# A bias table read back in four parts through GpSimd's queue, and key norm roots formed earlier

## The chip, the cores and the metric

The kernel runs on one core of one Trainium2 chip. The core has five engines that run side by side, each through its own list of instructions in a fixed order: TensorE (PE, matmuls; its weight loads are shown as PEld), VectorE (DVE), ScalarE (ACT), GpSimd (POOL) and SyncE (SP, which in this kernel only issues DMA transfers). They wait for one another by semaphores. The metric is device time in microseconds (us) of one launch, the median of three runs.

## The reference, cut to what matters

The program is a decoder trunk of two layers over 256 tokens of 1024 channels, all in float32. Layer 0 mixes tokens by a state-space scan (S5); then one set of keys and values is made; layer 1 mixes by attention that reads them. Around each mixer stand two feed-forward blocks (SwiGLU), four in all:

```python
for layer in range(DEPTH):                       # DEPTH = 2
    h = h + 0.5 * swiglu(rmsnorm(h, ffn1_norm), w_in, w_out)
    h = h + mixer(rmsnorm(h, mix_norm))          # S5 in layer 0, attention in layer 1
    h = h + 0.5 * swiglu(rmsnorm(h, ffn2_norm), w_in, w_out)
    if layer == 0:
        kv = rmsnorm(h, kv_norm) @ w_kv          # (256, 6, 4, 64)
        k_cmp = rmsnorm(compress(kv[:, 0])); v_cmp = compress(kv[:, 1])
        k_slc = rmsnorm(kv[:, 2]); k_win = rmsnorm(kv[:, 4])   # v: kv[:, 3], kv[:, 5]
```

Attention adds to its logits a bias that depends only on the head (16) and on the distance of two tokens, `rel_bias[bucket(distance), head]`, and masks negative distances.

## The kernel before, in words

**Weights.** Every product is a float32 product done in three passes (lines 126 to 128): weights are loaded as 1 MB granules `raw` (line 76, always on SP, two buffers), ScalarE writes the rounded part `whi` (line 92 without, line 105 with a gain) and VectorE the rest `wlo` (lines 96 and 108). Each granule is two halves; five halves of `whi` and five of `wlo` have room. A `raw` buffer is free for the next load when VectorE has read it for the last time, and a half is free when TensorE has done with it.

**A feed-forward block** (`ffn`) goes through 11 chunks of 256 hidden columns. In each TensorE does 48 passes of 512 columns into `mm` (two granules of `w_in`), four transposes of the previous chunk's `g` (line 265, into a bank `tr` that ScalarE and VectorE empty into `turned`, lines 151 and 152), then ScalarE and VectorE form `g` (lines 306 and 307) and TensorE does 24 passes into `o` with one granule of `w_out`. From the second such chunk on this is a period of 72 passes.

**Background work.** Four times in a chunk and once after it, `background` lets a generator go on by one step; a step may say with `yield 4` that it counts for four. In the second feed-forward block of layer 0 the generators are `kv_consts` and `bias_tables`; in the first of layer 1 it is `post`, which makes the transposed keys. The order in which the instructions of such a block stand on each engine is set when the kernel is built, by a scheduler with its own estimate of every instruction and transfer; it is fixed at run time. Only the S5 part and the attention have an order written out by hand.

**The bias table.** `bias_tables` makes `rev`, for 128 rows a reversed table of 384 distances (line 833, a matmul with one-hot rows; lines 835 and 836). It writes `rev` twice to a scratch `revd` in DRAM (line 840), and reads it back eight times with a step that shifts each row by one (line 846), into `B` (128 x 16 heads x 256). Both are issued by SP, between the loads of `raw`. `B` is first read in the attention (line 1153).

**The keys.** `post` first transposes the compressed branch's inputs `kd` in four steps (line 917: four transposes each, emptied by VectorE at line 919 and by ScalarE at line 921 or 923). Then, for the two other branches (`n` = 1, 2) and two halves of the tokens (`t`), it squares `kt` on GpSimd (`sq`, line 853), sums on VectorE (`hss`, 855), scales (`hms`, 861), takes the root on GpSimd (`hrr`, 863), multiplies on VectorE (`kn`, 929), applies the gain on GpSimd (`kd2`, shown as `kd`, 932) and transposes (936). `sq`, `kn` and `kd2` have one buffer each; `hss`, `hms` and `hrr` have one too.

Of the kernel before, what the change touches and what calls it, by code (L numbers as in the profile page):

```python
# [9 lines left out]
F32 = mybir.dt.float32  # L10
# [6 lines left out]
P = 128  # L17
# [6 lines left out]
EPS = 1e-6  # L24
# [8 lines left out]
def kernel(ctx: ExitStack, tc: tile.TileContext, A, out):  # L33
# [791 lines left out]
    def bias_tables(kp, tp):  # L825

        rb = tp.tile([32, P], F32, name="rb")
        nc.sync.dma_start(out=rb, in_=A["rel_bias"])
        oh = tp.tile([32, 256], F32, name="oh")
        nc.sync.dma_start(out=oh, in_=A["bucket"])  # L830
        yield
        ps = tr_bank()
        T.matmul(ps[:, 0:256], lhsT=rb, rhs=oh, start=True, stop=True)
        rev = tp.tile([P, 384], F32, name="rev")
        G.memset(rev[:, 256:384], -1e30)
        V.tensor_copy(rev[:, 0:256], ps[:, 0:256])
        yield
        dr = dscr.tile([16, 16, 384], F32, name="revd")
        for r in range(2):
            nc.sync.dma_start(out=dr[8 * r:8 * r + 8].rearrange("q h k -> (q h) k"), in_=rev)  # L840
            yield
        yield
        KV.B = kp.tile([P, 16, 256], F32, name="B")
        for r in range(8):
            src = bass.AP(tensor=dr.tensor, offset=dr.offset + 127 - 16 * r, ap=[[16 * 384 - 1, 16], [384, 16], [1, 256]])
            nc.sync.dma_start(out=KV.B[16 * r:16 * r + 16], in_=src)
            yield 4

    def head_ss(tp, x, nh):

        rows = x.shape[0]
        sq = tp.tile([P, 384], F32, name="sq")[:rows, :nh * 64]
        G.tensor_tensor(out=sq, in0=x, in1=x, op=ALU.mult)
        ss = tp.tile([P, 8], F32, name="hss")[:rows, :nh]
        V.tensor_reduce(out=ss, in_=sq.rearrange("p (h d) -> p h d", d=64), axis=mybir.AxisListType.X, op=ALU.add)
        return ss

    def inv_sqrt(tp, ss, scale, eps):
        rows, n = ss.shape
        ms = tp.tile([P, 8], F32, name="hms")[:rows, :n]  # L860
        V.tensor_scalar(out=ms, in0=ss, scalar1=scale, scalar2=eps, op0=ALU.mult, op1=ALU.add)
        rr = tp.tile([P, 8], F32, name="hrr")[:rows, :n]
        G.tensor_tensor(out=rr, in0=ms, in1=nhalf[:rows, :n], op=ALU.pow)
# [18 lines left out]
    def shared_kv(x, kp, tp):  # L882
# [26 lines left out]
        def post():  # L909
            w1 = tp.tile([P, 16, P], F32, name="cw1")  # L910
            nc.sync.dma_start(out=w1, in_=A["cmp_k_w1"])
            kvT = KV.kvT
            for t in range(2):
                for i in range(2):
                    ps = tr_bank()
                    for g in range(4):
                        T.transpose(ps[:, g * P:(g + 1) * P], kd[t][:, i * 4 + g].rearrange("p a d -> p (a d)"), ident)
                    pv = ps.rearrange("p (g c) -> p g c", g=4)
                    V.tensor_copy(kvT[i][0:64, 0:4, t * P:(t + 1) * P], pv[0:64])
                    if t == 0:  # L920
# [4 lines left out]
            for n in (1, 2):  # L925
                for t in range(2):
                    rr = inv_sqrt(tp, head_ss(tp, kt[n, t], 4), 1.0 / 64, EPS)
                    kn = tp.tile([P, 4, 64], F32, name="kn")
                    V.tensor_tensor(out=kn, in0=kt[n, t].rearrange("p (g d) -> p g d", g=4), in1=rr.unsqueeze(2).to_broadcast([P, 4, 64]), op=ALU.mult)
                    kd2 = tp.tile([P, 4, 2, 64], F32, name="kd2")  # L930
# [43 lines left out]
            yield  # L974
            rr = inv_sqrt(tp, head_ss(tp, kc, 1), 1.0 / 64, EPS)
            kcd = tp.tile([60, 2, 64], F32, name="kcd")
            for u in range(2):
# [421 lines left out]
def _arrays(np, I):  # L1399
# [20 lines left out]
    A["w_glu"] = _w_out(I["s5_w_glu"][0])  # L1420
    A["rel_bias"] = np.tile(I["rel_bias"], (1, 8))
    n = np.arange(255, -1, -1)
# [47 lines left out]
```

## Time and profile before

| what | value |
|---|---|
| median of three runs | 998.76 us (998.57 to 1000.18) |
| the profiled execution's own time | 1000.22 us |
| its span in the trace | 998.5 us |
| TensorE busy, of the span | 969.4 us (97%) |
| VectorE, ScalarE, GpSimd busy | 659.0, 577.1, 80.6 us |
| granted TensorE clock | full (2.4 GHz) over the whole span |
| DMA moved | 168.96 MB, mean 169 GB/s |

The profile shows one execution; its own time stands 1.46 us over the median, and its span 1.72 us under its own time. Matmuls overlap in the records (each is shown with 0.39 us, and the next starts 0.23 us after it), so a busy TensorE is not one at its peak: what tells a slow stretch is the length of a chunk, and the idle time ahead of single weight loads. Stretches are given in us from the span's start: the second feed-forward block of layer 0 lies at some 270 to 460, the keys' product and the first block of layer 1 at 460 to 700, the attention at 700 to 820.

### The profile page before, as it was taken

To read this page: it belongs to the slowest core of one execution; us is meant where nothing else is said; L and a number is where in the kernel's file an instruction comes from. 1 tells how busy PE (TensorE), PEld (TensorE's weight loads), DVE (VectorE), ACT (ScalarE), POOL (GpSimd) and SP (SyncE) were. 2 spreads that over 40 slices of the span, in tenths; PEclk is the share of its full clock that TensorE was granted. 3 is DMA by queue.
4 is the path that set the end of the run, shared out by engine and by line. 5 is a ranking of instruction groups with operands and counts; after the bars stand their busy time and mean duration, and the time that the engine had idled before them with its cause. 6 is when DMAs were issued, how large, how long until landed. Compare 5 with 4: busy or idle time off the path is not lost.

```text
span 998.5 us, 14337 instructions
## 1 busy us (share of the span) xinstructions
PE 969.4 (97%) x5523; PEld 794.1 (80%) x5523; DVE 659.0 (66%) x1210; ACT 577.1 (58%) x1023; POOL 80.6 (8%) x91
## 2 busy tenths in 40 slices
PE   6999999999999989999999999999988999999998
PEld 5788788788878867788878888888876778888886
DVE  4998875579964544657566556565899676555553
ACT  5677666463663543656656545454888565555552
POOL 3001012312200000000032000000200000000000
PEclk9999999999999999999999999999999999999999
DMA  7555565433357556564644445554431235555551
GB/s 270 192 192 202 174 208 177 164 94 146 97 190 212 158 174 216 185 228 151 248 169 166 170 171 197 182 189 135 127 107 43 85 127 211 193 186 185 195 179 74
DMA packets 28948, 168.96 MB, mean 169 GB/s; under 512 B 4560, under 2 KB 7184, under 8 KB 10064
## 3 DMA queue, kind: packets, MB, share of 16 engines
q1 hardware_dynamic: 28656, 167.26, 49.7%
q8 instruction: 43, 0.70, 0.3%
q0 software_dynamic: 224, 0.79, 0.2%
q14 instruction: 25, 0.20, 0.1%
HBM read 165.54 MB, written 2.49 MB: 168 GB/s over the span
## 4 chain that ended last, share of the span: by engine, by line
PE 78%; DVE 11%; ACT 5%; DMA 4%; issue 1%; POOL 1%; SPq 0%; ACTq 0%
PE mm L126 15%; PE mm L127 15%; PE mm L128 14%; PE o L128 7%; PE o L127 7%; PE o L126 7%; DMA raw<-in_w_in_dram 3%; DVE wlo L96 3%; PE tr L265 2%; ACT whi L92 1%; DVE Pt L1153 1%; PE dr L596 1%; PE tr L945 1%; PE ga L126 1%; PE ga L128 1%
## 5 line engine op out<-in xcount | busy, mean ns | idle before, releaser
L126 PE MATMUL mm<-whi,xT 128*128 128x512 f32 (+2 forms) x800 | 312.4, 392 | 6.1 <-ACT whi L92 2.6
L127 PE MATMUL mm<-wlo,xT 128*128 128x512 f32 (+2 forms) x800 | 306.3, 383 | 0.7 <-DVE wlo L96 0.5
L128 PE MATMUL mm<-whi,xT 128*128 128x512 f32 (+2 forms) x800 | 305.9, 383 | 0.0
L108 DVE SCALAR_TENSOR_TENSOR wlo<-raw,gains,whi 128x512 fp32r<-128x512 f32 x274 | 192.7, 748 | 86.7 <-ACT whi L105 84.1
L105 ACT ACTIVATE whi<-raw,gains 128x512 fp32r<-128x512 f32 x274 | 182.6, 718 | 98.8 <-PE mm L128 50.1
L96 DVE TENSOR_TENSOR wlo<-raw,whi 128x1024 fp32r<-128x1024 f32 x132 | 160.5, 1224 | 104.4 <-ACT whi L92 103.8
L92 ACT ACTIVATE whi<-raw 128x1024 fp32r<-128x1024 f32 x132 | 138.4, 1059 | 121.5 <-PE mm L128 51.5
L126 PEld LDWEIGHTS mm<-whi,xT 128*128 128x128 f32 x800 | 150.7, 189 | 37.1 <-ACT whi L105 3.1
L127 PEld LDWEIGHTS mm<-wlo,xT 128*128 128x128 f32 x800 | 151.1, 189 | 29.4 <-DVE wlo L96 1.5
L128 PEld LDWEIGHTS mm<-whi,xT 128*128 128x128 f32 x800 | 150.7, 188 | 29.3
L128 PE MATMUL o<-whi,turned 128*128 128x512 f32 x352 | 137.5, 391 | 0.8 <-DVE turned L152 0.8
L127 PE MATMUL o<-wlo,turned 128*128 128x512 f32 x352 | 137.6, 391 | 0.1
L126 PE MATMUL o<-whi,turned 128*128 128x512 f32 x352 | 136.8, 391 | 0.0
L128 PEld LDWEIGHTS o<-whi,turned 128*128 128x128 f32 x352 | 66.1, 188 | 15.0 <-DVE turned L152 1.5
L127 PEld LDWEIGHTS o<-wlo,turned 128*128 128x128 f32 x352 | 66.1, 188 | 14.4 <-DVE wlo L96 1.0
L126 PEld LDWEIGHTS o<-whi,turned 128*128 128x128 f32 x352 | 66.0, 188 | 13.7
L306 ACT ACTIVATE g<-mm,rs 128x256 f32<-128x256 f32 x88 | 41.0, 472 | 45.2 <-PE mm L128 44.9
L307 DVE SCALAR_TENSOR_TENSOR g<-mm,rs,g 128x256 f32<-128x256 f32 x88 | 41.7, 482 | 36.2 <-ACT g L306 36.1
L152 DVE TENSOR_TENSOR turned<-tr,turned 128x512 fp32r<-128x512 f32 x44 | 30.3, 688 | 36.1 <-ACT turned L151 35.7
L151 ACT ACTIVATE turned<-tr 128x512 fp32r<-128x512 f32 x44 | 26.1, 593 | 45.9 <-PE tr L265 45.9
L148 POOL TENSOR_TENSOR rs<-ms,nhalf 128x1 f32<-128x1 f32 x12 | 7.6, 633 | 284.4 <-DVE ms L147 284.4
L1160 ACT ACTIVATE Pt<-Pt,mx 128x128 f32<-128x128 f32 (+1 forms) x64 | 28.3, 446 | 3.7 <-DVE mx L1153 3.7
(321 smaller groups left out, 982.0 us busy)
## 6 DMA issues: line engine op xcount, KB each, us to landing
raw<-in_w_in_dram SPq DMA_DIRECT2D x87, 1024.0 KB, 4.9
raw<-in_w_out_dram SPq DMA_DIRECT2D x44, 1024.0 KB, 4.9
raw<-in_w_kv_dram SPq DMA_DIRECT2D x6, 1024.0 KB, 4.8
raw<-in_w_glu_dram SPq DMA_DIRECT2D x4, 1024.0 KB, 4.9
raw<-in_w_o_dram SPq DMA_DIRECT2D x4, 1024.0 KB, 5.0
raw<-in_w_qg_dram SPq DMA_DIRECT2D x6, 512.0 KB, 3.6
B<-revd SPq DMA_DIRECT2D x8, 256.0 KB, 7.5
raw<-in_w_qg_dram SPq DMA_DIRECT2D x2, 608.0 KB, 3.8
```

What stands on the lines that cost most here:

```text
L92: Last.act = S.activation(hi, r, AF.Copy)
L96: Last.dve = V.tensor_tensor(out=lo, in0=r, in1=hi.bitcast(F32), op=ALU.subtract)
L105: Last.act = S.activation(hi[:, c], r[:, c], AF.Identity, scale=g_)
L108: i = V.scalar_tensor_tensor(out=lo[:, c], in0=r[:, c], scalar=g_, in1=hi[:, c].bitcast(F32), op0=ALU.mult, op1=ALU.subtract)
L126: T.matmul(ps, lhsT=xh, rhs=wh, start=start, stop=False)
L127: T.matmul(ps, lhsT=xh, rhs=wl, start=False, stop=False)
L128: Last.pe = T.matmul(ps, lhsT=xl, rhs=wh, start=False, stop=stop_)
L151: i = S.activation(dst_hi, src, AF.Copy)
L152: V.tensor_tensor(out=dst_lo, in0=src, in1=dst_hi.bitcast(F32), op=ALU.subtract)
L306: Last.act = S.activation(sl, acc[t][:, 0:256], AF.Silu, scale=rs[:, t:t + 1])
L307: Last.dve = V.scalar_tensor_tensor(out=g[:, t, :], in0=acc[t][:, 256:512], scalar=rs[:, t:t + 1], in1=sl, op0=ALU.mult, op1=ALU.mult)
L1160: S.activation(p_, p_, AF.Exp, scale=-1.0, bias=mx[g, t][:, c:c + 1], accum_out=sm[g, t][:, c:c + 1])
```

## The change

Three edits, the first in `bias_tables`:

```diff
-        dr = dscr.tile([16, 16, 384], F32, name="revd")
-        for r in range(2):
-            nc.sync.dma_start(out=dr[8 * r:8 * r + 8].rearrange("q h k -> (q h) k"), in_=rev)
-            yield
-        yield
         KV.B = kp.tile([P, 16, 256], F32, name="B")
-        for r in range(8):
-            src = bass.AP(tensor=dr.tensor, offset=dr.offset + 127 - 16 * r, ap=[[16 * 384 - 1, 16], [384, 16], [1, 256]])
-            nc.sync.dma_start(out=KV.B[16 * r:16 * r + 16], in_=src)
-            yield 4
+        for n in range(4):
+            dr = dscr.tile([16, 4, 384], F32, name=f"revd{n}")
+            for q in range(2):
+                nc.sync.dma_start(out=dr[8 * q:8 * q + 8].rearrange("q h k -> (q h) k"), in_=rev[32 * n:32 * n + 32])
+            for r in range(8):
+                src = bass.AP(tensor=dr.tensor, offset=dr.offset + 127 - 16 * r, ap=[[4 * 384 - 1, 16], [384, 4], [1, 256]])
+                nc.gpsimd.dma_start(out=KV.B[16 * r:16 * r + 16, 4 * n:4 * n + 4], in_=src)
+                yield
```

The scratch becomes four scratches of four heads each. Each is written by two transfers of 48 KB on SP and read back by eight transfers of 64 KB on GpSimd's queue: 8 writes and 32 reads in place of 2 writes and 8 reads, with the same bytes. The rows of `rel_bias` are put in the order that this needs when the inputs are prepared. The second edit is in `post`, and gives `hss`, `hms` and `hrr` four buffers (`bufs=4`):

```diff
-            kvT = KV.kvT
+            kvT, root = KV.kvT, {}
             for t in range(2):
                 for i in range(2):
+                    root[i + 1, t] = inv_sqrt(tp, head_ss(tp, kt[i + 1, t], 4), 1.0 / 64, EPS)
                     ps = tr_bank()
...
-                    V.tensor_copy(kvT[i][0:64, 0:4, t * P:(t + 1) * P], pv[0:64])
+                    placed = V.tensor_copy(kvT[i][0:64, 0:4, t * P:(t + 1) * P], pv[0:64])
...
-                    rr = inv_sqrt(tp, head_ss(tp, kt[n, t], 4), 1.0 / 64, EPS)
                     kn = tp.tile([P, 4, 64], F32, name="kn")
-                    V.tensor_tensor(out=kn, in0=kt[n, t].rearrange("p (g d) -> p g d", g=4), in1=rr.unsqueeze(2).to_broadcast([P, 4, 64]), op=ALU.mult)
+                    with tc.issue_after(placed.ins):
+                        V.tensor_tensor(out=kn, in0=kt[n, t].rearrange("p (g d) -> p g d", g=4), in1=root[n, t].unsqueeze(2).to_broadcast([P, 4, 64]),
+                                        op=ALU.mult)
```

The four roots are formed in the four steps of the first transposes, and every `kn` stands behind the last `kvT` copy. The third edit adds one `yield` between the root of the compressed key and the products that use it, so that its transpose comes a step later.

As the scheduler sets the order, the change moves other instructions too. The first place is ScalarE's list in the second feed-forward block of layer 0, three chunks from the third row of `g` (L306) on. Before:

```order
L306 ACTIVATE g<-mm,rs 128x256 x2
L105 ACTIVATE whi<-raw,gains 128x512 x4
L151 ACTIVATE turned<-tr 128x512
L105 ACTIVATE whi<-raw,gains 128x512 x4
L92 ACTIVATE whi<-raw 128x1024 x2
L306 ACTIVATE g<-mm,rs 128x256 x2
L151 ACTIVATE turned<-tr 128x512
L105 ACTIVATE whi<-raw,gains 128x512 x8
L306 ACTIVATE g<-mm,rs 128x256 x2
L92 ACTIVATE whi<-raw 128x1024 x2
L151 ACTIVATE turned<-tr 128x512
L105 ACTIVATE whi<-raw,gains 128x512 x8
```

The same place now:

```order
L306 ACTIVATE g<-mm,rs 128x256 x2
L105 ACTIVATE whi<-raw,gains 128x512 x4
L92 ACTIVATE whi<-raw 128x1024 x2
L105 ACTIVATE whi<-raw,gains 128x512 x2
L151 ACTIVATE turned<-tr 128x512
L105 ACTIVATE whi<-raw,gains 128x512 x2
L306 ACTIVATE g<-mm,rs 128x256 x2
L105 ACTIVATE whi<-raw,gains 128x512 x4
L92 ACTIVATE whi<-raw 128x1024 x2
L105 ACTIVATE whi<-raw,gains 128x512 x2
```

The order now has one pattern for every chunk, the same as in the other feed-forward blocks; before, `turned` (L151) stood at another place in almost every chunk, ahead of up to eight `whi`. VectorE's list follows ScalarE's line by line.

The second place is SP's list in the same block, from the first write of the scratch on (`raw` are the weight granules):

```order
-L840 DMA revd<-rev 128x384 x2
+L842 DMA revd_3058<-rev 32x384 x2
 L76 DMA raw<-in_w_in_0_dram 128x2048
-L846 DMA B<-revd 16x16x256 x2
+L842 DMA revd_3256<-rev 32x384 x2
+L76 DMA raw<-in_w_out_0_dram 128x2048
+L76 DMA raw<-in_w_in_0_dram 128x2048 x2
 L76 DMA raw<-in_w_out_0_dram 128x2048
 L76 DMA raw<-in_w_in_0_dram 128x2048
-L846 DMA B<-revd 16x16x256
+L842 DMA revd_3470<-rev 32x384 x2
 L76 DMA raw<-in_w_in_0_dram 128x2048
```

The reads of `B` have left this list; the four writes of the scratch stand apart from each other.

The third place is VectorE's list in the first block of layer 1, from the second `g` of its first chunk on (here with the buffers' numbers, since rows read alike without them). Before:

```order
L307 SCALAR_TENSOR_TENSOR g_4603<-mm_4526,rs_4188,g_4603 128x256
L919 COPY kvT0_2925<-tr_4610 64x4x128
L855 TENSOR_REDUCE hss_4725<-sq_4723 128x4
L96 TENSOR_TENSOR wlo_4744<-raw_4741,whi_4743 128x1024
L861 TENSOR_SCALAR hms_4727<-hss_4725 128x4
L919 COPY kvT1_2926<-tr_4639 64x4x128
L929 TENSOR_TENSOR kn_4731<-kt__4423,hrr_4729 128x256
L96 TENSOR_TENSOR wlo_4760<-raw_4741,whi_4759 128x1024
L855 TENSOR_REDUCE hss_4784<-sq_4782 128x4
L861 TENSOR_SCALAR hms_4786<-hss_4784 128x4
L929 TENSOR_TENSOR kn_4790<-kt__4426,hrr_4788 128x256
L919 COPY kvT0_2925<-tr_4664 64x4x128
```

The same place now, from the row behind that `g` on:

```order
L854 TENSOR_REDUCE hss_4645<-sq_4643 128x4
L919 COPY kvT0_2925<-tr_4651 64x4x128
L860 TENSOR_SCALAR hms_4647<-hss_4645 128x4
L854 TENSOR_REDUCE hss_4682<-sq_4680 128x4
L96 TENSOR_TENSOR wlo_4801<-raw_4798,whi_4800 128x1024
L860 TENSOR_SCALAR hms_4684<-hss_4682 128x4
L919 COPY kvT1_2926<-tr_4688 64x4x128
L854 TENSOR_REDUCE hss_4715<-sq_4713 128x4
L96 TENSOR_TENSOR wlo_4817<-raw_4798,whi_4816 128x1024
L860 TENSOR_SCALAR hms_4717<-hss_4715 128x4
L854 TENSOR_REDUCE hss_4757<-sq_4755 128x4
L860 TENSOR_SCALAR hms_4759<-hss_4757 128x4
```

The next row now is the third `kvT` copy. Two `kn` have gone from ahead of it to behind the fourth one, and two more pairs of `hss` and `hms` stand ahead of it.

## Rows read from the trace of the kernel before

**Rows 1.** The page: busy time of each engine over the span, and the share of each engine in the chain of work that ended last.

```profile
PE 969.4 (97%) x5523; PEld 794.1 (80%) x5523; DVE 659.0 (66%) x1210; ACT 577.1 (58%) x1023; POOL 80.6 (8%) x91
PE 78%; DVE 11%; ACT 5%; DMA 4%; issue 1%; POOL 1%; SPq 0%; ACTq 0%
```

**Rows 2.** Busy time by stretch, each stretch one chunk from the second `g` on ScalarE to the next chunk's: the stretch and its length, busy us (and instructions) of each engine, granted clock, mean DMA share, GB/s. Six chunks of the second block of layer 0, and one of the first block of layer 1.

```profile
327.82:344.63 16.81, 16.81 (x77) 13.86 (x76) 9.53 (x14) 8.48 (x14) 0.00 (x0) 1.00 0.47 160
344.63:363.36 18.73, 17.38 (x77) 13.86 (x76) 9.43 (x14) 8.47 (x14) 0.00 (x0) 1.00 0.73 203
363.36:382.08 18.72, 17.33 (x76) 13.48 (x74) 6.96 (x12) 6.45 (x11) 0.00 (x0) 1.00 0.58 201
382.08:400.56 18.48, 17.66 (x76) 13.82 (x76) 9.32 (x14) 8.36 (x13) 0.00 (x0) 1.00 0.71 195
400.56:419.06 18.50, 17.72 (x77) 14.19 (x78) 11.69 (x16) 10.37 (x16) 0.00 (x0) 1.00 0.63 205
419.06:435.87 16.81, 16.81 (x77) 13.91 (x76) 12.04 (x18) 10.93 (x18) 0.00 (x0) 1.00 0.61 217
603.76:620.55 16.79, 16.79 (x77) 13.91 (x76) 9.78 (x14) 8.94 (x14) 0.00 (x0) 1.00 0.54 188
```

**Rows 3.** Timeline of the weight loads in the long chunks, those with idle time ahead of them: start, us, engine, line, operation, output and input, count, and in brackets the idle time and what ended it.

```profile
357.21 0.30 PEld L126 LDWEIGHTS mm<-whi,xT 128*128 128x128 f32 x2 [1.53 <-ACT whi L105]
357.99 0.19 PEld L127 LDWEIGHTS mm<-wlo,xT 128*128 128x128 f32 x1 [0.49 <-DVE wlo L108]
...
382.45 0.14 PEld L265 LDWEIGHTS tr<-ident,g 128*128 128x128 f32 x1 [0.83 <-DVE g L307]
```

**Rows 4.** Timeline of ScalarE in the first two of the long chunks, columns as in rows 3.

```profile
347.19 2.57 ACT L105 ACTIVATE whi<-raw,gains 128x512 fp32r<-128x512 f32 x4 [2.09 <-DMA raw<-in_w_in_dram]
355.95 0.60 ACT L151 ACTIVATE turned<-tr 128x512 fp32r<-128x512 f32 x1 [6.19 <-PE tr L265]
356.44 2.56 ACT L105 ACTIVATE whi<-raw,gains 128x512 fp32r<-128x512 f32 x4
```

**Rows 5.** The reads of `B` and the transfers: the instructions of line 846 from 299 to 400 us (duration min/median/max in ns, first and last start), and from the page the issues by tile (count, KB each, median us from issue to landing).

```profile
L846 SPq DMA_DIRECT2D B<-revd x8: 383/425/441, 305.2 to 395.7; - x8
...
raw<-in_w_in_dram SPq DMA_DIRECT2D x87, 1024.0 KB, 4.9
...
B<-revd SPq DMA_DIRECT2D x8, 256.0 KB, 7.5
...
WBT<-in_s_b_dram POOLq DMA_DIRECT2D x1, 512.0 KB, 7.4
...
revd<-rev SPq DMA_DIRECT2D x2, 192.0 KB, 4.4
```

**Rows 6.** Timeline of GpSimd: the only two transfers that it issues, and its first instruction behind the second block of layer 0.

```profile
7.60 0.74 POOL L435 DMA_DIRECT2D WBT<-in_s_b_dram  x1
8.35 0.55 POOL L436 DMA_DIRECT2D WBT<-in_s_gain_dram  x1
...
469.94 0.55 POOL L148 TENSOR_TENSOR rs<-ms,nhalf 128x1 f32<-128x1 f32 x1 [191.94 <-DVE ms L147]
```

**Rows 7.** A chunk of the first block of layer 1: SP's loads in the timeline, the use of a `w_out` granule by ScalarE, and the time from issue to landing (min/median/max) of the loads of line 76 from 586 to 690 us, then of those from 299 to 320 us.

```profile
587.13 0.33 SPq L76 DMA_DIRECT2D raw<-in_w_out_dram  x1
...
593.09 1.06 ACT L92 ACTIVATE whi<-raw 128x1024 fp32r<-128x1024 f32 x1 [1.38 <-PE o L128]
...
DMA to landing us min/median/max: 3.6/4.8/5.1
...
DMA to landing us min/median/max: 5.7/5.9/7.5
```

**Rows 8.** Timeline of VectorE in the first block of layer 1, from the second `g` of its first chunk on.

```profile
511.48 0.68 DVE L919 COPY kvT<-tr 64x512 f32<-64x512 f32 x1
512.08 0.40 DVE L855 TENSOR_REDUCE hss<-sq 128x4 f32<-128x256 f32 x1
512.41 1.21 DVE L96 TENSOR_TENSOR wlo<-raw,whi 128x1024 fp32r<-128x1024 f32 x1
...
515.27 0.42 DVE L929 TENSOR_TENSOR kn<-kt__4423,hrr 128x256 f32<-128x256 f32 x1 [0.54 <-POOL hrr L863]
...
517.20 0.27 DVE L861 TENSOR_SCALAR hms<-hss 128x4 f32<-128x4 f32 x1
519.71 0.43 DVE L929 TENSOR_TENSOR kn<-kt__4426,hrr 128x256 f32<-128x256 f32 x1 [2.25 <-POOL hrr L863]
520.05 0.68 DVE L919 COPY kvT<-tr 64x512 f32<-64x512 f32 x1
```

**Rows 9.** Timeline of GpSimd in the same stretch.

```profile
512.63 1.49 POOL L853 TENSOR_TENSOR sq<-kt__4426 128x256 f32<-128x256 f32 x1 [24.12 <-DVE hss L855]
514.22 1.02 POOL L863 TENSOR_TENSOR hrr<-hms,nhalf 128x4 f32<-128x4 f32 x1
515.78 2.36 POOL L932 TENSOR_TENSOR kd<-kn,kg 128x256 f32<-128x256 f32 x2 [0.54 <-DVE kn L929]
518.09 0.61 POOL L853 TENSOR_TENSOR sq<-kt__4507 128x256 f32<-128x256 f32 x1
```

**Rows 10.** The weight load of the fourth set of transposes, and ScalarE's part of the third copy, in the timelines of these two.

```profile
521.41 0.42 PEld L917 LDWEIGHTS tr<-ident,kd 128*128 128x128 f32 x4 [1.73 <-ACT kvT L923]
...
520.76 0.60 ACT L923 ACTIVATE kvT<-tr 64x512 f32<-64x512 f32 x1 [2.86 <-DVE kvT L919]
```

More of the change, by code (lines that the diff above doesn't have):

```diff
@@ L853, in head_ss @@
         G.tensor_tensor(out=sq, in0=x, in1=x, op=ALU.mult)
-        ss = tp.tile([P, 8], F32, name="hss")[:rows, :nh]
+        ss = tp.tile([P, 8], F32, name="hss", bufs=4)[:rows, :nh]
         V.tensor_reduce(out=ss, in_=sq.rearrange("p (h d) -> p h d", d=64), axis=mybir.AxisListType.X, op=ALU.add)
@@ L859, in inv_sqrt @@
         rows, n = ss.shape
-        ms = tp.tile([P, 8], F32, name="hms")[:rows, :n]
+        ms = tp.tile([P, 8], F32, name="hms", bufs=4)[:rows, :n]
         V.tensor_scalar(out=ms, in0=ss, scalar1=scale, scalar2=eps, op0=ALU.mult, op1=ALU.add)
-        rr = tp.tile([P, 8], F32, name="hrr")[:rows, :n]
+        rr = tp.tile([P, 8], F32, name="hrr", bufs=4)[:rows, :n]
         G.tensor_tensor(out=rr, in0=ms, in1=nhalf[:rows, :n], op=ALU.pow)
@@ L975, in post @@
             rr = inv_sqrt(tp, head_ss(tp, kc, 1), 1.0 / 64, EPS)
+            yield
             kcd = tp.tile([60, 2, 64], F32, name="kcd")
@@ L1420, in _arrays @@
     A["w_glu"] = _w_out(I["s5_w_glu"][0])
-    A["rel_bias"] = np.tile(I["rel_bias"], (1, 8))
+    A["rel_bias"] = np.tile(I["rel_bias"].reshape(32, 4, 1, 4), (1, 1, 8, 1)).reshape(32, 128)
     n = np.arange(255, -1, -1)
```

## The prediction, made before the result was known

> **What bounds the kernel now.** The page comes first: TensorE is busy for 97% of the span and carries 78% of the chain that ended last [rows 1]. A change can gain only where TensorE waits or starts late; the other engines' time is free unless TensorE comes to wait for it. As a busy TensorE is no proof of its pace, I next cut the feed-forward blocks into chunks and compared lengths [rows 2]. An undisturbed chunk takes 16.79 us. In the block that reads the bias table back, the chunks at 327.82 and 419.06 take 16.81, but the four between them take 18.73, 18.72, 18.48 and 18.50, together 74.43. Four undisturbed ones are 4 x 16.79 = 67.16, so 7.27 us are lost there, with the granted clock at full speed in all of them.
>
> Then the timeline of the weight loads, to see what TensorE waited for. In the first long chunk it is whi for 1.53 us and wlo for 0.49; in the third it begins with 0.83 on g [rows 3]. ScalarE's timeline tells why: it ended four whi at 349.76, then stood 6.19 us in front of turned, waiting for TensorE's transposes of g, with four more whi behind that instruction [rows 4]. These began at 356.44, which is where TensorE ran dry. So it is the fixed order, not the transfers, that makes these waits. The order listing agrees: before, turned stands ahead of up to eight whi, and at another place in almost every chunk.
>
> The second loss lies in the first block of layer 1. TensorE's fourth set of transposes waited 1.73 us for ScalarE's part of the third kvT copy, which had waited for VectorE's part [rows 10]; VectorE had stood 2.25 us before the second kn, for a root on GpSimd [rows 8].
>
> **The change part by part.** *The order of the second block of layer 0.* With the reads of B off SP's list, every chunk has the order of the chunk of 16.79 us. Term: -7.27 us. From both sides: at best each long chunk falls to 16.79, which is that figure; at worst the new order stalls as the old one did and the term is 0. I take 7.27, because the pattern is the one whose length a row shows.
>
> *SP's list.* The eight reads leave it: 8 x 0.425 = 3.4 us of SP's time [rows 5], and none of TensorE's waits [rows 3] is for a transfer. Six more writes come: at that price 2.6 us. The first write waits for rev as before; the loads of raw behind it are the same. I take 0.
>
> *GpSimd's list.* 32 transfers are issued there. The two that the trace shows took 0.74 and 0.55 us to issue [rows 6], so 17.6 to 23.7 us in all. Nothing else stands on GpSimd until the norm of the next block at 469.94, after 191.94 us of idling [rows 6], so there is room. The first write of the scratch goes out at about 300 us, a little ahead of the first read of B at 305.2 [rows 5]; the last one stands eleven loads later in SP's list, which at three loads per chunk of 16.79 is 62 us, at 362. Each part waits for its write, 4.4 us as before [rows 5], and then come eight issues of at most 0.74 us and a landing of 7.4 us [rows 5]: 18 us for a part. So the last part is done at 380, 90 us early. B is first used in the attention. Cost 0 on the path; without that cover the norm would come late by what is missing.
>
> *The loads of raw beside the parts.* The bytes are the same, but a part now comes beside the loads on a queue of its own. Undisturbed, a load lands in 4.8 us; beside the reads of B, from 299 to 320 us, in 5.7 to 7.5 [rows 7]. The margin: a granule issued at 587.13 lands some 4.8 later, at 591.9, and is first read at 593.09, 1.2 us later [rows 7]. Behind that stand the halves of whi and wlo already made. The nearest row is the chunk at 327.82, which follows those slow loads and still took 16.81 [rows 2]. So 0 here; the other bound is in the rivals. Below nothing it cannot go, since the chunk at 16.79 has no wait left to lose.
>
> The Trainium skill ("DMA: Bandwidth & Descriptors", section "Issuing engines are not separate DMA queues") speaks against the change: transfers from any engine run on the same 16 DMA engines, and a second issuing engine saves only the time of issuing. By that rule alone the first edit would be worth nothing, since SP's issue time bounds no chunk here; what the rule would do with the whole sum stands with the third rival.
>
> *The roots.* Time from the second g to the third kvT copy on VectorE. Before: the first kvT began at 511.48 and the third at 520.05 [rows 8]. Now there stand ahead of the third: two kvT of 0.68, four hss of 0.40, two wlo of 1.21 and four hms of 0.27, in all 6.46; from 511.48 that gives 517.9 if nothing waits. Two kn (0.42 and 0.43) and the waits 0.54 and 2.25 go. New waits: each hss wants a sq, and there is one buffer for it. Between the second hss and the third, GpSimd takes a root (1.02) and a sq (0.61, or 1.49 beside a wlo [rows 9]): 1.6 to 2.5 us; VectorE has 1.21 + 0.27 + 0.68 = 2.2 us of work meanwhile. Between the third and the fourth, again a root and a sq, part of them already done, against 1.5 us of work. So VectorE waits 0 to 0.3, then 0 to 1.0 us, and the third copy begins at 517.9 to 519.2, 0.8 to 2.1 us earlier. TensorE's wait of 1.73 falls by as much, at most to nothing. I take 1.5, nearer the full wait, as only the sq beside a wlo is the slow one. Behind it the second kn waits for GpSimd's products of the first (2.36 us for two [rows 9]) against 0.7 of wlo, so g comes late by at most 1.7 us. TensorE has 24 passes into o to do in between, some 5.6 us at the pace of a chunk (72 passes in 16.79, transposes included). That covers it. The bounds of this term: a gain of 1.73, and a loss of the same size if VectorE's new waits outgrow the old ones.
>
> The Trainium skill ("SBUF — State Buffer", section "Who interferes with whom") says that a VectorE instruction with two SBUF inputs, as wlo is, and a GpSimd one that reads SBUF shut each other out. The trace agrees where sq took 1.49 us beside a wlo and 0.61 alone [rows 9]; with every sq so slowed this term would be 0.8 and the time 0.7 us longer.
>
> *The yield* moves one small transpose by a step: 0.
>
> Sum: 7.27 + 1.5 = 8.8 us. The profiled execution took 1000.22 us (span 998.5), so one like it would take 991.4. It stands 1.46 above the median of the runs; taken from that median, 998.76 - 8.8 = 990.0 us.
>
> **The rivals.** *The roots gain nothing.* VectorE's waits for sq and roots are as long as the one removed: 998.76 - 7.3 = 991.5; at the bound of a loss of 1.7 it is 993.2. For it: four sq through one buffer, on an engine that shared badly with wlo. Against: what VectorE does between them is about as long.
>
> *The bursts cost part of it.* The first two writes stand one load apart in SP's list, so 16 issues fall into one chunk or two. If VectorE stood still while GpSimd issues, 16 x 0.74 = 11.8 us would come on top of its 9.78 us of work in a chunk of 16.79 [rows 2]: 4.8 us too many, once. The other parts add 5.9 to 9.78, which fits. That gives 992.3 to 994.8, say 993.5. For it: no row shows a GpSimd transfer beside wlo. Against: VectorE is idle for 7 us of a chunk.
>
> *The change doesn't do what it says.* The long chunks come from B's bytes, which stay, and not from the order: a load did make ScalarE wait 2.09 us in the first of them [rows 4]. Then only the roots gain: 998.76 - 1.5 = 997.3. This is where the skill's rule on issuing engines leads if the order is no cause. Against: the chunk at 327.82 ran beside or right behind slow loads without loss, and the wait at 355.95 was for transposes with no load in sight.
>
> *Slower: the reads starve the loads.* A part is in flight for some 5.9 + 7.4 = 13 us, in which up to three loads are issued (three in 16.79). If each lands in 7.5 instead of 4.8 and nothing is caught up, each is 2.7 - 1.2 = 1.5 late: 4.5 per part, 18 for four, and the time is 990.0 + 18 = 1008. It decides from 8.8 / 4 = 2.2 us per part on. For it: the new queue is not behind the loads but beside them. Against: ScalarE and VectorE idle for 7 us or more in each chunk, in which they catch up.
>
> **How the numbers follow.** Chances: the forecast 0.56, the roots gain nothing 0.17, the bursts 0.15, no effect of the order 0.07, slower 0.05. The forecast's own range is 989.0 to 991.5: with 0.8 to 1.73 for the roots the sum gives 990.7 to 989.8, and the runs of before spread by 1.6, half of it to each side. The range for 8 in 10 takes in the first two rivals above, and half a microsecond below, for waits elsewhere that an earlier arrival may shorten: 988.5 to 995.5. A measurement here can tell some 0.2%, 2 us. The forecast and the first two rivals are faster by more than that, 0.88; no effect of the order is within it, 0.07; the starved loads are slower, 0.05.
>
> **What would show it.** Right: every chunk from 311 to 453 us at 16.8, no idle time of ScalarE ahead of turned above 1 us, GpSimd's issues at under 0.8 us and done before 385, and the fourth set of transposes with under 0.4 us of wait. Wrong: chunks of over 17 us where a part is in flight, with a wait for raw or wlo (bursts or starved loads); long chunks at the same places (bytes, not order); or a VectorE that waits for sq ahead of the third kvT copy.

## The result, and the profile after

The changed kernel takes 989.69 us (median of 4 runs, 988.65 to 991.26) against 998.66 for the kernel before in the same comparison (4 runs, 998.27 to 1000.18): a ratio of 0.9909, with a 95% interval of 0.9897 to 0.9921. It is 9.0 us faster; 8.8 had been forecast. The profiled execution of after took 989.46 us; its span is 987.7, 10.8 us shorter than that of before. Of this 1.0 us lies ahead of the second block of layer 0, where the change edits nothing (the first g of its second chunk stands at 310.36 us before and at 309.37 after); the four executions of before alone spread by 1.9.

The page of after, the two lines that answer to [rows 1]:

```profile
PE 964.6 (98%) x5523; PEld 793.6 (80%) x5523; DVE 662.1 (67%) x1210; ACT 580.6 (59%) x1023; POOL 95.9 (10%) x123
PE 82%; DVE 9%; ACT 5%; DMA 2%; issue 1%; POOL 0%; SPq 0%; DVEq 0%; ACTq 0%
```

Busy time by stretch in after, the chunks of the second block of layer 0 that answer to [rows 2] (stretch and length, busy us and instructions of PE, PEld, DVE, ACT, POOL, granted clock, DMA share, GB/s):

```profile
326.84:343.62 16.78, 16.78 (x77) 13.90 (x76) 9.76 (x14) 8.93 (x13) 4.05 (x8) 1.00 0.72 220
343.62:360.41 16.79, 16.79 (x77) 13.90 (x76) 9.77 (x14) 8.94 (x14) 0.00 (x0) 1.00 0.56 193
360.41:377.20 16.79, 16.79 (x77) 13.90 (x76) 9.77 (x14) 8.94 (x14) 4.05 (x8) 1.00 0.75 225
377.20:393.98 16.78, 16.78 (x77) 13.91 (x76) 9.76 (x14) 8.93 (x13) 0.00 (x0) 1.00 0.55 188
393.98:410.77 16.79, 16.79 (x77) 13.90 (x76) 9.77 (x14) 8.94 (x14) 0.00 (x0) 1.00 0.54 187
```

Every chunk is now the undisturbed one, the two with eight GpSimd issues in them too (POOL 4.05 us): TensorE's busy time is the whole length of each. The four long chunks of [rows 2] held 7.27 us more than that. ScalarE's timeline, against the 6.19 us of [rows 4]:

```profile
339.51 0.60 ACT L151 ACTIVATE turned<-tr 128x512 fp32r<-128x512 f32 x1 [0.46 <-PE tr L265]
356.30 0.60 ACT L151 ACTIVATE turned<-tr 128x512 fp32r<-128x512 f32 x1 [0.46 <-PE tr L265]
```

It reaches turned 0.46 us before the transposes are through. GpSimd's timeline shows the four parts and the first instruction behind them, where [rows 6] has 191.94 us of idling:

```profile
303.33 4.14 POOL L845 DMA_DIRECT2D B<-revd  x8 [26.32 <-DMA revd<-rev]
311.47 4.05 POOL L845 DMA_DIRECT2D B<-revd  x8 [4.01 <-DMA revd<-rev]
337.87 4.05 POOL L845 DMA_DIRECT2D B<-revd  x8 [22.34 <-DMA revd<-rev]
366.31 4.05 POOL L845 DMA_DIRECT2D B<-revd  x8 [24.40 <-DMA revd<-rev]
461.60 0.56 POOL L148 TENSOR_TENSOR rs<-ms,nhalf 128x1 f32<-128x1 f32 x1 [91.24 <-DVE ms L147]
```

Each part waits for its own write, which stands in SP's list; so SP's list spaces the parts 8 to 28 us apart. From the page, the reads' count, size and median time from issue to landing, against 7.5 us for 256 KB in [rows 5]:

```profile
B<-revd POOLq DMA_DIRECT2D x32, 64.0 KB, 5.0
```

In the first block of layer 1, VectorE's timeline from the second g on, as in [rows 8]:

```profile
503.13 0.41 DVE L854 TENSOR_REDUCE hss<-sq 128x4 f32<-128x256 f32 x1
503.45 0.67 DVE L919 COPY kvT<-tr 64x512 f32<-64x512 f32 x1
504.05 0.27 DVE L860 TENSOR_SCALAR hms<-hss 128x4 f32<-128x4 f32 x1
...
505.80 0.58 DVE L860 TENSOR_SCALAR hms<-hss 128x4 f32<-128x4 f32 x1
...
509.48 0.68 DVE L919 COPY kvT<-tr 64x512 f32<-64x512 f32 x1
...
512.87 0.41 DVE L929 TENSOR_TENSOR kn<-kt__4456,hrr 128x256 f32<-128x256 f32 x1
...
515.28 0.42 DVE L929 TENSOR_TENSOR kn<-kt__4459,hrr 128x256 f32<-128x256 f32 x1 [1.34 <-POOL kd L933]
```

The third copy, at 509.48, begins 6.35 us after the first row behind the second g (503.13, now an hss); before it was 8.57 (520.05 - 511.48 in [rows 8], where that row is the first copy). No kn stands ahead of it, and VectorE waits for no sq. The fourth transposes in the timeline of the weight loads have no wait any more, against 1.73 us in [rows 10]:

```profile
511.39 0.59 PEld L917 LDWEIGHTS tr<-ident,kd 128*128 128x128 f32 x4
```

From the first g of this block to that of its third chunk it is 37.89 us now (499.28 to 537.17 on ScalarE), where before took 39.77 (507.63 to 547.40): 1.9 less, the 1.73 and a little in the next chunk, where two waits of 0.27 us for VectorE went too. So 7.3 and 1.9 us are gone from the two places named, 9.2 in the profiled executions, beside 9.0 between the medians.

### The profile page after: what moved, and what is told of

Read it like the earlier page. It is cut to its first block, busy times and chain, and to the rows that moved or that the text cites. A ratio compares the mean times of both kernels' runs of the same rounds, so it can differ in the third digit from the quotient of the medians.

```text
span 987.7 us, 14395 instructions
## 1 busy us (share of the span) xinstructions
PE 964.6 (98%) x5523; PEld 793.6 (80%) x5523; DVE 662.1 (67%) x1210; ACT 580.6 (59%) x1023; POOL 95.9 (10%) x123
## 4 chain that ended last, share of the span: by engine, by line
PE 82%; DVE 9%; ACT 5%; DMA 2%; issue 1%; POOL 0%; SPq 0%; DVEq 0%; ACTq 0%
PE mm L126 15%; PE mm L127 15%; PE mm L128 15%; PE o L128 7%; PE o L126 7%; PE o L127 7%; DVE wlo L96 2%; PE tr L265 2%; DVE Pt L1155 1%; ACT whi L92 1%; PE dr L596 1%; DMA raw<-in_w_in_dram 1%; PE tr L946 1%; PE tr L167 1%; PE ga L126 1%
## 5 line engine op out<-in xcount | busy, mean ns | idle before, releaser
L105 ACT ACTIVATE whi<-raw,gains 128x512 fp32r<-128x512 f32 x274 | 184.1, 719 | 109.5 <-PE mm L128 65.4
L126 PEld LDWEIGHTS o<-whi,turned 128*128 128x128 f32 x352 | 66.1, 188 | 14.5 <-ACT turned L151 0.9
L306 ACT ACTIVATE g<-mm,rs 128x256 f32<-128x256 f32 x88 | 41.2, 472 | 30.6 <-PE mm L128 30.3
L151 ACT ACTIVATE turned<-tr 128x512 fp32r<-128x512 f32 x44 | 26.2, 595 | 20.3 <-PE tr L265 20.2
L265 PEld LDWEIGHTS tr<-ident,g 128*128 128x128 f32 x176 | 21.8, 139 | 5.8
```

What stands on the lines that cost most here:

```text
L105: Last.act = S.activation(hi[:, c], r[:, c], AF.Identity, scale=g_)
L126: T.matmul(ps, lhsT=xh, rhs=wh, start=start, stop=False)
L265: T.transpose(ps[:, (f * 2 + t) * P:(f * 2 + t + 1) * P], g[:, t, f * P:(f + 1) * P], ident)
L306: Last.act = S.activation(sl, acc[t][:, 0:256], AF.Silu, scale=rs[:, t:t + 1])
```

## The experiments

Two theories on the first term. *Order*: the long chunks came from what stands behind turned in ScalarE's list, or from where the transposes stand in TensorE's; which queue reads B doesn't matter. *Transfer*: they came from the reads themselves, by SP's queue, by the size of a read, or by the bytes beside the loads. On the second term: the gain is from the early roots, or from kn being held behind the copies. Lines of a kernel can be one or two off those of after.

| run | what it is | us, median | ratio to before, 95% |
|---|---|---|---|
| bias_only | first edit alone | 991.57 | 0.9926, 0.9913 to 0.9940 |
| roots_only | the rest alone | 997.33 | 0.9985, 0.9976 to 0.9995 |
| sp_spaced | before, wider steps | 991.38 | 0.9926, 0.9914 to 0.9938 |
| whole_on_pool | after, one scratch | 1002.41 | 1.0037, 1.0023 to 1.0050 |
| pinned | after, whi held behind turned | 992.09 | 0.9919, 0.9904 to 0.9934 |
| sp_at_once | before, no steps | 997.67 | 0.9979, 0.9969 to 0.9990 |
| double_reads | after, reads twice | 990.00 | 0.9897, 0.9883 to 0.9912 |
| kn_behind | after, roots late, kn held | 990.14 | 0.9898, 0.9881 to 0.9914 |
| parts_at_once | after, parts not spaced | 990.03 | 0.9906, 0.9890 to 0.9921 |
| roots_free | after, kn not held | 992.94 | 0.9932, 0.9913 to 0.9950 |
| spaced_roots | sp_spaced and roots | 989.54 | 0.9901, 0.9886 to 0.9916 |
| parts_on_sp | after, reads on SP | 996.09 | 0.9968, 0.9953 to 0.9983 |

Before had medians of 999.3 in the three comparisons.

**Each half alone.** The edits are those of the change's diff.

> Edit 1 alone (the bias table in four parts, read through GpSimd's queue); the key norm as before. If the two edits add up: 998.7 less the 7.3 us of the second block of layer 0, so 991.4 (990.9 to 991.9), with every chunk between 311 and 443 us at 16.8 us and the fourth key transposes' wait of 1.7 us [rows 10] still there. If edit 1 needs edit 2, or brings part of what is put down to the roots: under 990.5 or over 992.5.

> Edits 2 and 3 alone (roots formed with the first transposes, the yield); the bias table as before. If the edits add up: 998.7 less 1.7, so 997.0 (996.5 to 997.5), with four chunks of 18.5 to 18.7 us as in [rows 2] and no wait at the fourth key transposes. If the roots gain nothing by themselves: 998.7.

Both came out as expected: 7.8 and 2.0 us below before, together 9.8 beside 9.0 for both at once, within the intervals. The third edit, one `yield`, stands in roots_only and was not tried alone. The timeline of the weight loads in bias_only keeps the old wait at the fourth transposes:

```profile
511.79 0.42 PEld L916 LDWEIGHTS tr<-ident,kd 128*128 128x128 f32 x4 [1.72 <-ACT kvT L922]
```

and in roots_only the waits of [rows 3] are still there, while the fourth transposes have none:

```profile
355.61 0.30 PEld L126 LDWEIGHTS mm<-whi,xT 128*128 128x128 f32 x2 [1.54 <-ACT whi L105]
356.40 0.19 PEld L127 LDWEIGHTS mm<-wlo,xT 128*128 128x128 f32 x1 [0.49 <-DVE wlo L108]
```

**Same queue, same size, another order.** Only the steps between the reads of before differ:

```diff
             nc.sync.dma_start(out=KV.B[16 * r:16 * r + 16], in_=src)
-            yield 4
+            if r != 6:
+                yield (7, 7, 7, 7, 6, 5, 0, 1)[r]
```

> The kernel before, with nothing changed but the number of steps between the eight reads of the bias table: one scratch, eight reads of 256 KB, all on SP's queue, roots as before. ScalarE's and VectorE's lists in the second block of layer 0 come out nearly as in the changed kernel (two w_out splits, then two w_in splits, then turned). Order theory: the chunks are 16.8 us, the gain of 7.3 us is there without GpSimd's queue and without the parts: 991.4, up to 993 for the block's last two chunks, whose order differs. Queue theory (reads in SP's queue hold up the weight loads): chunks with a read ahead of a load stay at 18.5 us or more, 998 to 999. Size theory (256 KB pieces land too slowly): the same, 998 to 999.

991.38: the whole first gain, with eight reads of 256 KB on SP's queue. Chunks by stretch:

```profile
309.04:325.82 16.78, 16.78 (x77) 13.91 (x76) 9.59 (x14) 8.70 (x13) 0.00 (x0) 1.00 0.66 204
325.82:342.61 16.79, 16.79 (x77) 13.90 (x76) 9.80 (x14) 8.93 (x13) 0.00 (x0) 1.00 0.64 203
342.61:359.40 16.79, 16.79 (x77) 13.90 (x76) 9.78 (x14) 8.94 (x14) 0.00 (x0) 1.00 0.55 188
```

Neither GpSimd's queue nor the four parts are needed for it. That leaves one doubt: the wider steps also thin the transfers out. The trace of before speaks to it: the granule whose whi stood behind turned in the first long chunk was issued at 344.19 and landed 7.5 us later, at 351.7; ScalarE stood in front of turned until 355.95 and came to that whi at 356.44 [rows 4]. So the data lay there for over 4 us. In the second long chunk ScalarE stood in front of turned until 369.2 with eight whi behind it; their granules had landed at 364.8 and 368.0. The next run makes such waits with no read at all.

**Another order, no reads.** In after, splits traced behind the transposes are held behind turned in four chunks that come after the last read:

```diff
-                split(gT[:, 0], gT[:, 1], ps.rearrange("p (f c) -> p f c", f=2))
+                Last.turned = split(gT[:, 0], gT[:, 1], ps.rearrange("p (f c) -> p f c", f=2))
...
-                        w = next(g_in)
+                        with ExitStack() as pin:
+                            if first and bg and 7 <= c <= 10 and k > 4:
+                                pin.enter_context(tc.issue_after(Last.turned.ins))
+                            w = next(g_in)
```

> The changed kernel, with the first-layer splits of the last half granule of a chunk (k of 6 and 7) held behind ScalarE's turned instruction in chunks 7 to 10 of the second block of layer 0, that is 376 to 443 us, when no read of the bias table is in flight any more (the last is issued at 370). Same bytes, same queues, another order on ScalarE: the whi of k 6 and 7 waits behind turned, which waits for the transposes. Order theory: these four chunks are 1 to 2 us longer each, as the 1.7 to 1.9 us of [rows 2], all others 16.8: 993.7 to 997.7. Transfer theory (the long chunks came from reads and loads that share the DMA engines): 989.7, chunks of 16.8.

992.09, that is 2.4 us over after, and the chunks, with no read of B in flight:

```profile
377.08:394.39 17.31, 17.25 (x77) 13.76 (x76) 6.06 (x9) 5.90 (x9) 0.00 (x0) 1.00 0.24 70
394.39:411.72 17.33, 17.28 (x77) 13.76 (x76) 9.35 (x14) 8.59 (x14) 0.00 (x0) 1.00 0.50 181
```

ScalarE stood 10.98 us ahead of turned there, and TensorE's weight loads waited for what was behind it:

```profile
391.02 0.30 PEld L126 LDWEIGHTS mm<-whi,xT 128*128 128x128 f32 x2 [0.35 <-ACT whi L105]
391.80 0.19 PEld L127 LDWEIGHTS mm<-wlo,xT 128*128 128x128 f32 x1 [0.49 <-DVE wlo L108]
```

It is the pair of waits of [rows 3], with 0.35 for 1.53. So order alone makes such a loss. Its size, 0.5 us a chunk, is under the 1 to 2 that were expected (and 992.09 under 993.7 to 997.7): here TensorE had six passes left between the transposes and the whi it lacked (389.48 to 391.02 in its timeline); before, the pass right behind the transposes was the one that lacked it. Those six passes took 1.54 us, about as much as 0.53 falls short of the 1.94 of the first long chunk of before (18.73 - 16.79). The loads also moved here: ScalarE holds raw longer, and the next two go out at 392.44 and 394.95. TensorE's waits in these chunks are for the held whi and its wlo alone, and the held whi begins right behind turned, without a wait for its load.

**The same parts on SP's queue.** `nc.gpsimd` becomes `nc.sync` in after's line 845.

> The changed kernel with its 32 reads of 64 KB issued on SP's queue instead of GpSimd's; roots as in the changed kernel. ScalarE's and VectorE's lists in the second block of layer 0 come out in yet another order, with turned ahead of splits in five or six chunks. Order theory: each of those is 0.5 to 1.9 us longer, 992 to 1000, and the long chunks are those with the odd order, wherever the reads lie. Transfer theory: the pieces and their pacing are as in the changed kernel, so 989.7 to 991.

996.09. Four chunks took 18.2 to 18.5 us from first g to first g, where five or six had been expected, all others 16.8. TensorE's waits from 290 to 560 us (total, times, longest):

```profile
PEld tr L265 <- DVE g L307: 3.8, 5, 0.8
PEld o L127 <- DVE wlo L96: 2.0, 4, 0.5
```

That is the other kind of long chunk, the third row of [rows 3]: the transposes stand right behind the chunk's last pass, so TensorE waits for g itself. These waits are for g and for w_out's split, none of them for a transfer. It is again the order, this time TensorE's. ScalarE did wait for loads in these chunks, 4.6 us at most, but TensorE never for what it makes of them by L105.

**What a burst costs.** After with one scratch and eight reads of 256 KB on GpSimd's queue; ScalarE's and VectorE's lists are after's:

```diff
-        for n in range(4):
-            dr = dscr.tile([16, 4, 384], F32, name=f"revd{n}")
...
+        dr = dscr.tile([16, 16, 384], F32, name="revd")
...
+        for r in range(8):
+            src = bass.AP(tensor=dr.tensor, offset=dr.offset + 127 - 16 * r, ap=[[16 * 384 - 1, 16], [384, 16], [1, 256]])
+            nc.gpsimd.dma_start(out=KV.B[16 * r:16 * r + 16], in_=src)
```

> The changed kernel with the table as one scratch again: two writes, then eight reads of 256 KB instead of 32 of 64 KB, on GpSimd's queue; roots as in the changed kernel. ScalarE's and VectorE's lists are the same as in the changed kernel. Order theory: 989.7, chunks of 16.8 us, at most 1.5 us more for one load that lands later beside the burst of 2 MB. Split theory (the four parts keep the loads from starving): 2 MB in one burst at the rate of a 1 MB load in 4.9 us hold a load by up to 9.8 us, one or two chunks are 3 to 8 us longer: 993 to 998.

1002.41, slower than before and over the ranges of both theories. All chunks but two are undisturbed, and these are

```profile
310.92:338.34 27.42, 18.23 (x79) 14.53 (x78) 8.59 (x13) 8.40 (x14) 0.00 (x0) 0.85 0.95 180
338.34:355.63 17.29, 17.29 (x75) 14.17 (x74) 10.41 (x16) 8.87 (x14) 0.00 (x0) 0.94 0.52 183
```

10.6 and 0.5 us too long. ScalarE's timeline shows the start of it, a w_out load that was issued at 310.39 and landed 19.0 us later:

```profile
329.46 2.00 ACT L92 ACTIVATE whi<-raw 128x1024 fp32r<-128x1024 f32 x2 [14.48 <-DMA raw<-in_w_out_dram]
```

TensorE waited 9.19 us for turned behind it:

```profile
336.85 0.80 PE L126 MATMUL o<-whi,turned 128*128 128x512 f32 x1 [9.19 <-ACT turned L151]
```

Its granted clock over the chunk was 0.85, so part of its passes ran at 1.2 instead of 2.4 GHz: the first behind the wait start some 0.43 us apart (338.41, 338.83, 339.26, 339.69 in its timeline), where 0.23 is usual, and from 340.41 on they are at 0.23 again. In the timeline of the queue all eight reads leave GpSimd in 4.55 us:

```profile
304.88 4.55 POOL L846 DMA_DIRECT2D B<-revd  x8 [27.02 <-DMA revd<-rev]
```

and the transfers of the same stretch, 280 to 345 us in 40 slices of 1.6 us, run at some 110 to 150 GB/s from 309 to 322 us, the load beside the reads included, against 380 and more in slices with loads alone:

```profile
DMA  5999148647747946699999999799999977912783
GB/s 96 383 378 408 35 60 323 262 60 282 303 60 282 374 170 81 272 376 124 121 116 113 129 111 141 151 247 197 222 197 189 257 192 194 418 40 30 257 358 50
```

Is that GpSimd's queue, the size of the pieces, or the pause between the parts? Three runs. First the same burst on SP: the `yield 4` of before becomes a single `yield` behind the last read.

> The kernel before with the eight reads of 256 KB issued in one go on SP's queue, between two weight loads (no steps between them); roots as before. Against the run with the same burst on GpSimd's queue, where one w_out load took 19.0 us to land and one chunk was 10.1 us longer. If it is the burst of 2 MB, on whichever queue: the load issued next lands 10 us late or more, one chunk is about 10 us longer, the others 16.8 but for two whose order differs: 991.4 + 10 = 1001 (998 to 1005). If it is GpSimd's queue that takes the DMA engines away from the loads: on SP the burst costs at most 3 us, 991 to 995.

997.67, 6.3 us over sp_spaced and just under the first theory's range. One chunk and the next took 39.98 us together, 6.4 too much:

```profile
327.65:367.63 39.98, 36.09 (x153) 29.08 (x154) 24.01 (x33) 21.99 (x32) 0.00 (x0) 0.96 0.62 229
```

The w_out load behind the burst landed 18.1 us after its issue, and the weight loads waited:

```profile
328.02 0.14 PEld L265 LDWEIGHTS tr<-ident,g 128*128 128x128 f32 x1 [0.83 <-DVE g L307]
...
332.36 0.49 PEld L126 LDWEIGHTS o<-whi,turned 128*128 128x128 f32 x2 [3.36 <-ACT whi L92]
333.62 0.29 PEld L127 LDWEIGHTS o<-wlo,turned 128*128 128x128 f32 x1 [0.77 <-DVE wlo L96]
```

So 2 MB at once hurt on either queue; the first of these waits is the order again. Whether GpSimd's queue adds something of its own (11.1 us there, 6.4 here) is not separated, as ScalarE's lists differ in two chunks.

Then the small pieces without the pauses: the four scratches of after are written first, and all 32 reads follow.

```diff
         for n in range(4):
-            dr = dscr.tile([16, 4, 384], F32, name=f"revd{n}")
             for q in range(2):
...
+        for n in range(4):
             for r in range(8):
```

> The changed kernel with the four scratches written one behind the other at the start, so that all 32 reads of 64 KB follow on GpSimd's queue with no wait between parts; ScalarE's and VectorE's lists as in the changed kernel. It stands against the run with one scratch, where eight reads of 256 KB in one burst cost one chunk 10.1 us. If the size of the pieces spares the loads (32 issues of 0.51 us spread 2 MB over 16.5 us, and a load lands between them): 989.7 to 992, no chunk over 18 but the one of 17.6. If it is the pause between the parts, which wait for their writes in SP's list: one load lands 8 to 14 us late, one chunk is 27 us: 997 to 1002.

990.03, no long chunk. GpSimd's timeline:

```profile
304.25 4.62 POOL L846 DMA_DIRECT2D B<-revd  x9 [26.29 <-DMA revd<-rev]
310.89 4.03 POOL L846 DMA_DIRECT2D B<-revd  x8 [2.01 <-DMA B<-revd]
317.42 4.03 POOL L846 DMA_DIRECT2D B<-revd  x8 [2.49 <-DMA B<-revd]
322.52 3.53 POOL L846 DMA_DIRECT2D B<-revd  x7 [1.07 <-DMA B<-revd]
```

An issue takes 0.51 us with 64 KB and 0.57 (4.55 / 8) with 256, so 32 issues are 16.3 us of work. Between them GpSimd waited three times for earlier pieces to land, 5.6 us in all, and the 2 MB leave in 21.8 us (304.25 to 326.05) instead of 4.55. The four loads issued meanwhile landed in 5.5 to 6.3 us. So small pieces are enough, and the long pauses between the parts aren't needed. How much is due to the time of an issue, and how much to GpSimd's own waits, is not separated.

Last, twice the bytes: each read of after is issued twice.

> The changed kernel with every one of the 32 reads issued twice, so bursts of 1 MB where the changed kernel has 0.5 MB and the run with one scratch had 2 MB (10.1 us lost). ScalarE's and VectorE's lists as in the changed kernel. If what a burst costs is its bytes less a margin of the loads: the burst of 2 MB was covered for 2 MB less what 10 us carry; 1 MB takes about half of its time, so 0 to 2 us per burst, 990 to 994 in all. If any burst beyond 0.5 MB holds a load up by its share: 2.5 to 5 us in each of the four bursts, 1000 to 1010. In either case chunks without a burst stay at 16.8.

990.00. It does not try what it was meant to, bursts of 1 MB: GpSimd waited again and again for earlier reads to land (up to 4.6 us), so that 64 reads went out over 82 us. It does show that 4 MB at that pace cost nothing; the loads from 296 to 380 us took

```profile
DMA to landing us min/median/max: 5.0/5.5/6.2
```

**Early roots, or a held kn.** In kn_behind the roots are formed where they were before, in the loop of the second transposes, and kn stays held:

```diff
-                    root[i + 1, t] = inv_sqrt(tp, head_ss(tp, kt[i + 1, t], 4), 1.0 / 64, EPS)
...
+                    root[n, t] = inv_sqrt(tp, head_ss(tp, kt[n, t], 4), 1.0 / 64, EPS)
```

> The changed kernel with the key norm roots formed where they were before (in the loop of the second key transposes), but kn still held behind the last of the four first copies. If the wait at the fourth key transposes [rows 10] was due to kn standing ahead of the third copy on VectorE, and the earlier roots bring nothing by themselves: no wait there, 989.7 (989 to 990.5). If the roots have to be early, or else kn is late at the second transposes: the 1.7 us come back there, 991.4.

In roots_free the roots are early and the `with tc.issue_after(placed.ins):` is gone.

> The changed kernel with kn no longer held behind the last of the four first copies; the roots early as in the change. VectorE's list then has two kn ahead of the third and fourth copies again. If it is the place of kn that makes the fourth key transposes wait [rows 8, 10]: the third copy is 0.4 to 1.6 us later than in the changed kernel, and the fourth transposes wait 0 to 1 us: 989.7 to 990.7. If early roots alone take the wait away: 989.7. If kn waits there for its root on GpSimd as before: 991.4.

kn_behind: 990.14, and no wait at the fourth transposes. roots_free: 992.94, worse than any of the three expectations. VectorE's timeline there has one kn ahead of the second copy, and a wait ahead of the third that is longer than the one the change removed:

```profile
505.79 0.82 DVE L929 TENSOR_TENSOR kn<-kt__4456,hrr 128x256 f32<-128x256 f32 x1 [0.69 <-POOL hrr L862]
...
512.06 0.42 DVE L854 TENSOR_REDUCE hss<-sq 128x4 f32<-128x256 f32 x1 [2.10 <-POOL sq L852]
512.39 0.67 DVE L919 COPY kvT<-tr 64x512 f32<-64x512 f32 x1
```

Once kn is made early, GpSimd's products of it stand ahead of the next sq, and the third copy is 8.91 us behind the first row after the second g (512.39 - 503.48), where before had 8.57 and after 6.35. The weight load of the fourth transposes:

```profile
513.75 0.42 PEld L917 LDWEIGHTS tr<-ident,kd 128*128 128x128 f32 x4 [2.06 <-ACT kvT L923]
```

From the first chunk of this block to the third (g at 499.63 and 539.38, in after at 499.28 and 537.17) it lost 1.9 us against after; the rest of the difference lies in the attention stage: 132.6 us from the last chunk of this block to the next, 130.9 in after. The other kernels had 130.8 to 131.8 there, but sp_spaced 133.2, so one execution can't tell whether the edit does this; it stays open. The second term's gain hangs on the hold, and early roots without it are worth nothing. The four buffers and the third edit's `yield` stand in both kernels: they give nothing without the hold, and the hold without them was not tried. In kn_behind TensorE's list differs in this stretch as well, which leaves open how much early roots matter where kn is held.

**The change without its new queue.** The wider steps of sp_spaced and the roots edits of the change:

> The eight reads of 256 KB on SP's queue with wider steps (as in the run with wider steps alone), and the roots edits of the change. If the two gains add up whatever the queue: 991.4 - 1.7 = 989.7 (989.0 to 990.4), the same as the changed kernel, with neither the parts nor GpSimd's queue. If the parts or GpSimd's queue bring something of their own: 990.5 or more.

989.54, the same as after within the intervals. No version tried beats after by more than can be told.

## Why the prediction was right

*The order of the second block, -7.27 us.* Right in place, size and cause. The stretches show 7.3 gone; sp_spaced shows it without a new queue, pinned shows such waits without reads of B, and whole_on_pool shows what order does not cover. "With the reads of B off SP's list" was too narrow: reads can stay there, if they stand so far apart that the scheduler leaves turned where it was. The rule cited from the Trainium skill ("DMA: Bandwidth & Descriptors", section "Issuing engines are not separate DMA queues") holds as far as these runs go: the move of spaced reads to GpSimd's queue brought nothing that wider steps on SP did not (989.69 beside 989.54). One reading of the third rival was too strong: there was a load in sight of the wait at 355.95 (w_out's, 350.73 to 356.39, and a read of B, 351.10 to 358.41), but neither brought what TensorE lacked; that had landed at 351.7.

*GpSimd's list, cost 0.* Right. An issue took 0.51 us where 0.55 to 0.74 had been taken, a landing 5.0 where 7.4 had; the last part was issued by 370.4.

*The loads beside the parts, cost 0.* Right for the parts, and the loads did slow as they had before: 5.8, 6.2 and 7.1 us (min, median, max) from 299 to 320 us against 5.7, 5.9 and 7.5 in [rows 7]. From 266 to 450 us ScalarE waited twice for w_out's and twice for w_in's, 2.6 us at most, TensorE never.

*The roots, -1.5 us.* The term measured 1.9, the full wait of 1.73 and a little behind it, so a bit more than its bound. The named cause held: "two kn and the waits 0.54 and 2.25 go". The mis-sized step is the new waits for sq, 0 to 0.3 and 0 to 1.0: there were none, though two of three sq were slow beside a wlo, 0.97 and 1.47 us against 0.62, as the section of the Trainium skill cited there ("SBUF — State Buffer", "Who interferes with whom") has it. VectorE's own work was long enough to cover them, partly because two hms took 0.58 and 0.57 for the 0.27 of [rows 8]; before had one of 0.60 too, at 513.54, which the sum passes over. The work ahead of the third copy came to 6.35 us where 6.46 was worked out. kn waits 1.34 us for GpSimd behind the copies, and the passes into o covered that as worked out.

*The rivals.* "The roots gain nothing" and "the bursts cost part of it" did not happen; roots_free is the first of them made real, with its new wait of 2.10 us for sq. "The change doesn't do what it says" falls with sp_spaced and pinned. "The reads starve the loads" got 0.05 for parts of 0.5 MB, and those starve nothing. But the mechanism exists: 2 MB in reads of 256 KB made the kernel slower than before. Its price was put at 1.5 us per late load; the load that was late took 19.0 us to land, and that burst cost 11.1 us.

## What to carry to other kernels

Where an in-order engine stands in front of an instruction, look at what is queued behind it: here one early turned held up splits that TensorE needed, and the two edits that put it back in place, a new queue with small parts and a few wider steps, were worth the same. Before a bulk transfer is moved to an idle queue, ask how fast that queue will let it go: here small pieces went out slowly and left the loads nearly alone, large ones left at once and held the loads up. And when work is done early so that a wait ends sooner, hold its consumer back too; by itself the early work only reorders the engines that serve it.

## What the runs showed of the hardware that was not expected

While the reads of B are under way in whole_on_pool, the DMA engines move some 110 to 150 GB/s at a busy share of 0.9 and more, where loads of 1 MB alone move at 380. So 2 MB of them hold the engines for 15 us and more (their median landing was 15.5 us on GpSimd's queue, 14.5 on SP's), and a load that is issued behind them lands after 18 to 19 us instead of 5. The same bytes in pieces of 64 KB over 21.8 us left the loads beside them at 5.5 to 6.3 us. Why the slower pace spares the loads so fully was not tried.

Small VectorE instructions stretch beside GpSimd's sq as well: in after hms took 0.17 us at 509.40, beside an hrr, and 0.58 at 505.80 beside an sq, and kn 0.41 in after but 0.82 beside an sq in roots_free.
